# Hybrid decoder block on one core: the gates' first columns and dt from the plain transposed x, 1/rms on their products

## The chip, the cores and the metric

The kernel runs on one core of one Trainium2 chip. The metric is device time in microseconds (us) of one execution; less is better. Five engines work beside each other, each on its own queue in order: TensorE (PE, matmuls), VectorE (DVE), ScalarE (ACT), GpSimd (POOL) and SyncE (SP, which here only issues DMAs). They meet through semaphores. TensorE's clock has two levels, 1.2 and 2.4 GHz; the profile gives the granted level as a share of the higher one.

## What is computed

The reference is one decoder layer for a sequence of 256 tokens with 1024 channels. Cut to what matters here:

```python
hn = rmsnorm(x, norm1_w)                 # x * rsqrt(mean(x^2) + eps) * norm1_w
proj = hn @ w_in                         # z, x/B/C, dt, q, k, v, gates
z, xbc_raw, dt_raw, q, k, v, g_raw = jnp.split(proj, IN_OFFSETS, axis=-1)
dt = softplus(dt_raw + dt_bias)          # per token and head (32 heads)
gates = jax.nn.sigmoid(g_raw + b_gate)   # 2 x 1024 columns
merged = g_ssd * (y_ssd @ w_ssd_proj) + g_att * (y_att @ w_att_proj)
```

`y_ssd` comes from a chunked state-space scan that needs `dt`, `y_att` from causal attention over the 256 tokens. Then follow an output projection, a convolutional feed-forward layer and a last normalisation. Since 1/rms is one factor per token, `rmsnorm(x, w) @ W` is the same as `(x * w) @ W` with each token's row of the product multiplied by 1/rms.

## The kernel before

All matmuls over weights are done in three parts to keep float32's precision: a weight tile is split into `hi` (ScalarE, line 93, a rounded copy) and `lo` (VectorE, line 94, the rest), an activation likewise into a pair, and PE adds hi·hi, hi·lo and lo·hi. The weights arrive as units of 1 MB (128 partitions, 8 slices of 256 columns) in an order fixed by the list `seq`; `load_to` issues the transfers on SP into three `raw` buffers, `next_unit` hands out unit i, requests unit i+2 and splits unit i+1. A unit of 256 output columns is 48 matmuls of 128x256 (`mm_unit`, lines 148 to 150). The gates are made in blocks of 512 columns from two units each: 48 matmuls of 128x512 with the tokens as rows (`mm_tok`, lines 165 to 167), cut in four quarters of 12 by `u_gate`, a generator that is stepped with `next(gate)`.

The start (lines 225 to 260): x comes in token layout in three transfers, ScalarE squares and sums it (line 244), VectorE makes 1/rms by Newton steps (`rms_rstd`, lines 180 to 191), puts it on the diagonal of a matrix `dg` (line 249), and PE transposes and scales x in one by 16 float32 matmuls with `dg` (line 254). The norm weight is put on by `scaled_pairs` (lines 218 and 220), and eight pairs `hn` come out. Before x is there PE runs 14 matmuls on ones (line 71).

The order of PE's work is the program's order. For the first group g = 0 it is: `u_bc(0)` (B and C columns, then convolution and SiLU), `dt_mm` (32 columns of dt, line 460), `u_x(0)`, `dt_chain` (softplus on VectorE, lines 474 to 495), `u_qk(0)`, `u_z(0)`, `dt_sums` (cumulative sums, line 499), the first quarter of the gates, `dt_turn` (line 507; the sums go out to DRAM and come back spread over all partitions as `acsB`), `s_cb(0)` (lines 345 to 359: the decay matrix `mx`), the other quarters of the gates with `s_xt(0)` between, and then group 1: `u_bc(1)`, `s_y(0)` (line 381, the first product with `mx`), `u_x(1)` and so on. ScalarE's, VectorE's and GpSimd's orders are set by a planner at compile time from priorities in program order and its own costs. GpSimd does next to nothing: some memsets, and two products at the end (line 727).

Of the kernel before, what the change touches and what calls it, by code (L numbers as in the profile page):

```python
# [8 lines left out]
F32 = mybir.dt.float32  # L9
# [3 lines left out]
ALU = mybir.AluOpType  # L13
PSUM = bass.MemoryType.PSUM
DRAM = bass.MemoryType.DRAM
PE_ONLY = {mybir.EngineType.PE}

# [18 lines left out]
WARM = 14  # L36


def block_kernel(tc, xtok_d, par_d, nf_d, con_d, rope_d, wdt_d, win_d, wgate_d, bg_d, watt_d, wssd_d, wout_d, wup_d, wdn_d, out_d):
# [3 lines left out]
    with st:  # L43
# [12 lines left out]
        wdt = const.tile([P, KD, NH], F32, name="wdt")  # L56
        con3 = con[:, 0 : 7 * P].rearrange("p (a b) -> p a b", b=P)
# [15 lines left out]
        def col(c):  # L73
            return par[:, c : c + 1]
# [10 lines left out]

        def split_unit(raw, nk=KD):

            halves = []
            for k0 in range(0, nk, 4):
                n = min(4, nk - k0)  # L90
                hi = wpool.tile([P, 4, 256], F32R, tag="hi", bufs=4, name="hi")
                lo = wpool.tile([P, 4, 256], F32R, tag="lo", bufs=4, name="lo")
                nc.scalar.activation(hi[:, :n], raw[:, k0 : k0 + n], AF.Copy)  # L93
                nc.vector.tensor_tensor(lo[:, :n], raw[:, k0 : k0 + n], hi[:, :n].bitcast(F32), op=ALU.subtract)  # L94
                halves.append((hi, lo, n))
            return halves
# [72 lines left out]
        def mm_tile():  # L169
            return ps_mm.tile([P, 2, T], F32, tag="mm", bufs=3, name="mm")  # L170
# [59 lines left out]
        XCUT = ((0, 0, D), (1, 0, D // 2), (1, D // 2, D))  # L230
        for c, a, b in XCUT:
            nc.sync.dma_start(xtok[:, c, a:b], xtok_d[:, c, a:b])
        nc.sync.dma_start(con[:, 0:P], con_d[:, 0:P])
        nc.sync.dma_start(par, par_d)
        load_to(1)
        nc.sync.dma_start(con[:, P:], con_d[:, P:])
        nc.sync.dma_start(wdt, wdt_d)
        nc.sync.dma_start(rope, rope_d)
        ssum = work.tile([P, 3], F32, name="ssum")
        rstd1 = work.tile([P, 2], F32, name="rstd1")  # L240
        with tc.high_priority():
            junk = inp.tile([P, D], F32, name="junk")
            for i, (c, a, b) in enumerate(XCUT):
                nc.scalar.activation(junk[:, a:b], xtok[:, c, a:b], AF.Square, accum_out=ssum[:, i : i + 1])
            rms_rstd(rstd1[:, 0:1], ssum[:, 0:1], 1.0 / D)
            rms_rstd(rstd1[:, 1:2], ssum[:, 1:2], 1.0 / D, more=ssum[:, 2:3])
            dg = inp.tile([P, 2, P], F32, name="dg")
            for c in range(2):
                nc.vector.tensor_scalar(dg[:, c], ident, rstd1[:, c : c + 1], None, op0=ALU.mult)
            xps = [ps_mm.tile([P, 2, T], F32, tag="mm", bufs=3, name="xps") for _ in range(2)]  # L250
            xps += [ps_s.tile([P, 2, T], F32, tag="at", bufs=2, name="xps") for _ in range(2)]
            for c in range(2):
                for k in range(KD):
                    nc.tensor.matmul(xps[k // 2][:, k % 2, c * P : c * P + P], xtok[:, c, k * P : k * P + P], dg[:, c],
                                     start=True, stop=True)
            hn = []
            for i in range(4):
                hn += scaled_pairs("hn", [xps[i][:, m] for m in range(2)], [col(C_N1 + 2 * i + m) for m in range(2)])
# [196 lines left out]
        def dt_mm():  # L455
            with tc.manual_schedule(engines=PE_ONLY):
                for k in range(KD):
                    for i in range(2):
                        j = NH * (k % 2 * 2 + i)
                        nc.tensor.matmul(ps_dt[j : j + NH, 0, :], wdt[:, k], hn[k][:, i, :].bitcast(F32),  # L460
                                         start=(k < 2), stop=(k >= KD - 2))
# [10 lines left out]
        def dt_chain():  # L472
# [3 lines left out]
            for c in range(2):  # L476
                nc.tensor.matmul(ps[:, 0, c * NH : c * NH + NH], dtp[:, c * P : c * P + P], sel, start=True, stop=True)
            nc.vector.tensor_tensor(r3(0), ps[:, 0, 0 : 2 * NH].rearrange("p (c h) -> p c h", c=2),
                                    b3(par[:, C_DTB : C_DTB + NH]), op=ALU.add)
# [45 lines left out]
        gates = const.tile([P, 2, 2 * D], F32, name="gates")  # L525

        def u_gate(j):

            cols = slice(512 * j, 512 * j + 512)
            ps = [mm_tile(), mm_tile()]  # L530
            for k0 in (0, 4):
                hv = next_unit()
                mm_tok(ps, hv[:1], hn, k0, KD)
                yield
                mm_tok(ps, hv[1:], hn, k0 + 2, KD)
                if not k0:
                    yield
            for c in range(2):
                gt = gates[:, c, cols]
                nc.vector.tensor_tensor(gt, flat(ps[c]), gt, op=ALU.add)  # L540
                nc.scalar.activation(gt, gt, AF.Tanh, scale=0.5)
            yield

        for g in range(NG):
            if g:
                u_bc(g)
                s_y(g - 1)
                u_x(g)
                a_s(g - 1)
            u_qk(g)  # L550
            if g == 0:
                for c in range(2):
                    tc.keep_in_program_order(nc.scalar.dma_start(gates[:, c], bg_d.partition_broadcast(P)))
                u_z(g)
                dt_sums()
                gate = u_gate(0)
                next(gate)
                dt_turn()
                load_acs(0)
                s_cb(g)  # L560
                next(gate)
                s_xt(g)
                next(gate)
                next(gate)
            elif g % 2:
                s_cb(g)
                s_st(g - 1)
                u_v(g)
                a_t(g - 1)
                u_z(g)  # L570
                s_xt(g)
                a_o(g - 1)
                s_pb(g - 1)
            else:
                s_cb(g)
                s_st(g - 1)
                u_z(g)
                a_t(g - 1)
                s_xt(g)
                gate = u_gate(g // 2)  # L580
# [246 lines left out]
```

## Time and profile before

| | us |
|---|---|
| median of 3 runs | 615.52 |
| lowest and highest run | 615.33, 616.99 |
| the profiled execution | 617.0 |
| its span, first to last instruction | 615.2 |
| PE busy in it | 595.5 |
| VectorE busy | 464.0 |
| ScalarE busy | 358.5 |
| GpSimd busy | 4.1 |

The profiled execution is as long as the highest of the three runs. 1.8 us of it lie outside its span. Matmuls are pipelined and their ends are modelled in the profile, so the pace of PE is better read from the distance of the starts than from the durations.

### The profile page before, as it was taken

How to read it: one execution, taken by the hardware profiler on the slowest of the kernel's cores; microseconds unless marked ns; L12 is line 12 of the kernel's file. 1: busy time of each engine (PE TensorE's matmuls, PEld its weight loads, DVE VectorE, ACT ScalarE, POOL GpSimd, SP SyncE). 2: the span in 40 equal slices, each digit the busy share in tenths (PEclk: the TensorE clock that was granted, in tenths of full speed). 3: DMA queues.
4: the chain of work that ended last, by engine and by line, in shares of the span. 5: the costliest groups of instructions: out<-in, count | busy, mean ns of one | idle time of the engine just before them, and what ended most of it. 6: DMA issues, size and time to landing. Idle time of an engine off the chain costs nothing.

```text
span 615.2 us, 10606 instructions
## 1 busy us (share of the span) xinstructions
PE 595.5 (97%) x4194; PEld 545.0 (89%) x4194; DVE 464.0 (75%) x896; ACT 358.5 (58%) x648; POOL 4.1 (1%) x8
## 2 busy tenths in 40 slices
PE   8998999999999999999999999998999999999994
PEld 7897899989999899988988788788999999998883
DVE  4876898968979698896986546667888888884633
ACT  5645967649586595855846333455555555553431
POOL 0000000000000000000000000000000000000100
PEclk8999999999999999999999999999999999999998
DMA  8667364464544555345363765544455455455611
GB/s 331 218 232 271 120 211 171 150 222 138 192 142 165 205 169 177 138 151 202 136 208 94 279 196 174 185 161 152 164 206 172 171 206 174 172 205 162 214 35 69
DMA packets 17746, 109.78 MB, mean 178 GB/s; under 512 B 2176, under 2 KB 2592, under 8 KB 5664
## 3 DMA queue, kind: packets, MB, share of 16 engines
q1 hardware_dynamic: 15120, 100.15, 46.8%
q10 hardware_dynamic: 2576, 8.95, 4.2%
q8 instruction: 33, 0.54, 0.3%
q14 instruction: 17, 0.14, 0.1%
HBM read 107.49 MB, written 1.08 MB: 176 GB/s over the span
## 4 chain that ended last, share of the span: by engine, by line
PE 93%; DVE 3%; ACT 2%; DMA 1%; issue 1%; DVEq 0%; ACTq 0%
PE mm L148 17%; PE mm L149 16%; PE mm L150 16%; PE mm L167 10%; PE mm L165 10%; PE mm L166 10%; PE py L381 2%; PE mm L327 1%; PE mm L329 1%; PE mm L328 1%; PE s_ps L410 1%; DVE lo L94 1%; PE po L447 1%; PE pt_ps L433 1%; PE pb L210 1%
## 5 line engine op out<-in xcount | busy, mean ns | idle before, releaser
L93 ACT ACTIVATE hi<-raw 128x1024 fp32r<-128x1024 f32 x186 | 195.9, 1060 | 184.1 <-PE mm L167 83.8
L94 DVE TENSOR_TENSOR lo<-raw,hi 128x1024 fp32r<-128x1024 f32 x186 | 226.6, 1226 | 90.8 <-ACT hi L93 90.6
L148 PE MATMUL mm<-hn,hi 128*128 128x256 f32 x512 | 147.3, 288 | 0.0
L149 PE MATMUL mm<-hn,hi 128*128 128x256 f32 x512 | 145.0, 283 | 0.4 <-DVE hn L220 0.4
L150 PE MATMUL mm<-hn,lo 128*128 128x256 f32 x512 | 144.8, 283 | 0.0
L148 PEld LDWEIGHTS mm<-hn,hi 128*128 128x128 f32 x512 | 98.0, 191 | 4.1 <-issue 3.6
L149 PE MATMUL mm<-xw,hi 128*128 128x256 f32 x352 | 99.7, 283 | 1.0 <-DVE xw L220 1.0
L148 PE MATMUL mm<-xw,hi 128*128 128x256 f32 x352 | 99.8, 283 | 0.6 <-ACT xw L218 0.6
L150 PE MATMUL mm<-xw,lo 128*128 128x256 f32 x352 | 99.6, 283 | 0.0
L149 PEld LDWEIGHTS mm<-hn,hi 128*128 128x128 f32 x512 | 98.1, 192 | 0.9 <-DVE hn L220 0.8
L150 PEld LDWEIGHTS mm<-hn,lo 128*128 128x128 f32 x512 | 98.1, 192 | 0.0
L149 PEld LDWEIGHTS mm<-xw,hi 128*128 128x128 f32 x352 | 67.6, 192 | 1.2 <-DVE xw L220 1.2
L148 PEld LDWEIGHTS mm<-xw,hi 128*128 128x128 f32 x352 | 67.6, 192 | 0.8 <-ACT xw L218 0.8
L150 PEld LDWEIGHTS mm<-xw,lo 128*128 128x128 f32 x352 | 67.6, 192 | 0.0
L272 DVE SCALAR_TENSOR_TENSOR cacc<-mm,par,cacc 128x255 f32<-128x255 f32 (+2 forms) x96 | 44.2, 475 | 3.0 <-ACT cacc L268 2.9
L165 PE MATMUL mm<-hi,act 128*128 128x512 f32 x88 | 34.2, 389 | 0.0
L166 PE MATMUL mm<-lo,act 128*128 128x512 f32 x88 | 34.2, 389 | 0.0
L167 PE MATMUL mm<-hi,act 128*128 128x512 f32 x88 | 34.2, 389 | 0.0
L166 PE MATMUL mm<-lo,hn 128*128 128x512 f32 x64 | 25.0, 391 | 1.7 <-DVE lo L94 1.7
L165 PE MATMUL mm<-hi,hn 128*128 128x512 f32 x64 | 25.8, 404 | 0.0
L165 PE MATMUL mm<-hi,yn 128*128 128x512 f32 x64 | 25.3, 396 | 0.0
L167 PE MATMUL mm<-hi,hn 128*128 128x512 f32 x64 | 25.1, 392 | 0.0
(170 smaller groups left out, 939.6 us busy)
## 6 DMA issues: line engine op xcount, KB each, us to landing
raw<-in_win_dram SPq DMA_DIRECT2D x35, 1024.0 KB
raw<-in_wup_dram SPq DMA_DIRECT2D x22, 1024.0 KB
raw<-in_wdn_dram SPq DMA_DIRECT2D x10, 1024.0 KB
raw<-in_wgate_dram SPq DMA_DIRECT2D x8, 1024.0 KB
raw<-in_wssd_dram SPq DMA_DIRECT2D x8, 1024.0 KB
acsB<-acsT_d ACTq DMA_DIRECT2D x8, 512.0 KB
raw<-in_watt_dram SPq DMA_DIRECT2D x4, 1024.0 KB
raw<-in_wout_dram SPq DMA_DIRECT2D x4, 1024.0 KB
```

The lines of the kernel that those rows point to most:

```text
L93: nc.scalar.activation(hi[:, :n], raw[:, k0 : k0 + n], AF.Copy)
L94: nc.vector.tensor_tensor(lo[:, :n], raw[:, k0 : k0 + n], hi[:, :n].bitcast(F32), op=ALU.subtract)
L148: nc.tensor.matmul(ps[m], wh, xh, start=a, stop=False)
L149: nc.tensor.matmul(ps[m], wh, xl, start=False, stop=False)
L150: nc.tensor.matmul(ps[m], wl, xh, start=False, stop=z)
L165: nc.tensor.matmul(o, xh, wh, start=(k0 + k == 0), stop=False)
L166: nc.tensor.matmul(o, xh, wl, start=False, stop=False)
L167: nc.tensor.matmul(o, xl, wh, start=False, stop=(k0 + k == nk - 1))
L210: nc.tensor.matmul(pb[:, 0, c * P : c * P + P], y[:, c : c + 1].to_broadcast([P, P]), ident, start=True, stop=True)
L272: nc.vector.scalar_tensor_tensor(acc[:, s:], src[:, m, : T - s], w(m, 3 - s), acc[:, s:], op0=ALU.mult, op1=ALU.add)
L327: nc.tensor.matmul(ps[:, c, :], xh, hi[:, kk], start=(k == 0 and c == 0), stop=False)
L381: nc.tensor.matmul(o, xt[:, c, r, :], rhs, start=(c == 0), stop=(c == 1))
```

## The change

PE's first work is now the first gate block, and the normalised x is made later. In detail:

- Transfers: the identity and the norm weight go out first, on ScalarE's queue. On SP come the first half of x's columns, the first gate unit in three parts, the second half of x, the second gate unit in two parts, then `wdt`, the other parameters, the other constants and `rope`. The two gate units stand at the front of `seq`.
- x is transposed plainly (`x_turn`), split with the norm weight alone on it (`x_split`, pairs `xr`), and ScalarE, VectorE and PE follow a written order there (`IN_ORDER`), in which the splits of x and of the gate units alternate (`w_split`), and the squares (`x_square`) and `rms_rstd` come late.
- The four quarters of gate block 0 and `dt_mm` use `xr`. 1/rms is put on by one operand of the VectorE instruction that adds the bias, for the gates and for dt (there two instructions instead of one).
- GpSimd adds hi and lo of `xr` back to full values (`norm1_full`, 8 additions of 128x256), and when 1/rms is there and PE has spread it over the partitions (`rms_bcast`), multiplies them by it (8 products of 128x256); `split_pair` then makes the pairs `hn` (`norm1`).
- The order of group 0 is gates, `dt_mm`, `dt_chain`, `u_bc(0)`, `dt_sums`, `u_x(0)`, `dt_turn`, `u_qk(0)`, `s_cb(0)`, `u_z(0)`, `s_xt(0)`. The gates' bias is loaded for 512 columns first and for the others later. The matmuls on ones go from 14 to 10.

```diff
-WARM = 14
+WARM = 10
...
+        for d, h in ((con[:, 0:P], con_d[:, 0:P]), (par[:, 0:C_NW], par_d[:, 0:C_NW])):
+            nc.scalar.dma_start(d, h)
...
+        nc.sync.dma_start(xhalf(xtok, 0), xhalf(xtok_d, 0))
+        for k0, k1 in ((0, 2), (2, 4), (4, 8)):
+            nc.sync.dma_start(raw0[:, k0:k1], seq[0][0][:, k0:k1])
+        nc.sync.dma_start(xhalf(xtok, 1), xhalf(xtok_d, 1))
+        for k in (0, 4):
+            nc.sync.dma_start(raw1[:, k : k + 4], seq[1][0][:, k : k + 4])
...
+        def x_split():
+            k = len(xr)
+            xr.extend(scaled_pairs("xr", [xps[k // 2][:, k % 2]], [col(C_N1 + k)]))
...
+        def w_split(u, k0, step):
+            hi, lo = split_tiles()
+            for k in range(0, 4, step):
+                x_split()
+                split_part(raws[u][:, k0 + k : k0 + k + step], hi[:, k : k + step], lo[:, k : k + step])
+            units[u].append((hi, lo, 4))
+
+        def norm1_full():
+            for k in range(KD):
+                nc.gpsimd.tensor_tensor(full[:, k], xr[k][:, 0, :].bitcast(F32),
+                                        xr[k][:, 1, :].bitcast(F32), op=ALU.add)
+
+        def norm1():
+            nc.scalar.activation(rb1, rms_bcast(rstd1), AF.Copy)
+            for k in range(KD):
+                nc.gpsimd.tensor_tensor(full[:, k], full[:, k], rb1, op=ALU.mult)
+                hn.append(new_pair("hn"))
+                split_pair(hn[k], full[:, k])
...
+                    nc.vector.scalar_tensor_tensor(gt, flat(ps[c]), rstd[:, c : c + 1], gt, op0=ALU.mult, op1=ALU.add)
...
         st.enter_context(tc.manual_schedule(engines=PE_ONLY))
-        u_bc(0)
+        gate = u_gate(0, xr, rstd1)
+        with tc.manual_schedule(engines=IN_ORDER):
+            x_turn(0)
+            units.extend(([], []))
+            w_split(0, 0, 2)
+            next(gate)
+            w_split(0, 4, 2)
+            x_turn(1)
+            next(gate)
+            x_square(0)
+            w_split(1, 0, 4)
+            x_split()
+            x_square(1)
+            w_split(1, 4, 4)
+            x_split()
+            rms_rstd(rstd1, ssum[:, 0], 1.0 / D, more=ssum[:, 1])
+        load_bias(0, 512)
+        norm1_full()
         dt_mm()
-        u_x(0)
+        next(gate)
         dt_chain()
+        norm1()
+        next(gate)
...
+            else:
+                u_bc(0)
+                dt_sums()
+                u_x(0)
+                dt_turn()
+                load_acs(0)
             u_qk(g)
             if g == 0:
+                load_bias(512, 2 * D)
+                s_cb(g)
                 u_z(g)
-                dt_sums()
-                gate = u_gate(0)
-                next(gate)
-                dt_turn()
-                load_acs(0)
-                s_cb(g)
-                next(gate)
                 s_xt(g)
-                next(gate)
-                next(gate)
```

## Rows read from the trace of the kernel before

**Rows 1.** The page's first part: busy time of each engine, its share of the span and its instructions.
```profile
PE 595.5 (97%) x4194; PEld 545.0 (89%) x4194; DVE 464.0 (75%) x896; ACT 358.5 (58%) x648; POOL 4.1 (1%) x8
```

**Rows 2.** Busy time by stretches of the first 70 us. Columns: the stretch and its length; busy us and instructions of PE, PEld, DVE, ACT, POOL; the granted clock of TensorE; the mean busy share of the DMA engines; GB/s.
```profile
0.00:5.00 5.00, 3.95 (x18) 3.95 (x19) 0.17 (x1) 1.49 (x2) 0.20 (x4) 1.00 0.58 168
5.00:10.00 5.00, 3.01 (x20) 2.82 (x19) 3.42 (x25) 3.66 (x8) 0.00 (x0) 0.86 1.03 395
8.60:12.00 3.40, 3.40 (x17) 3.40 (x17) 2.43 (x9) 0.84 (x1) 0.00 (x0) 0.50 1.06 420
10.00:15.00 5.00, 5.00 (x35) 4.82 (x35) 2.67 (x5) 2.44 (x6) 0.00 (x0) 0.80 1.04 428
15.00:20.00 5.00, 4.61 (x39) 4.41 (x38) 5.00 (x9) 3.42 (x7) 0.00 (x0) 1.00 0.75 272
20.00:25.00 5.00, 5.00 (x59) 3.94 (x58) 3.59 (x7) 3.60 (x6) 0.00 (x0) 1.00 0.65 210
25.00:30.00 5.00, 5.00 (x44) 5.00 (x43) 3.92 (x7) 2.82 (x5) 0.99 (x2) 1.00 0.62 203
30.00:40.00 10.00, 10.00 (x86) 10.00 (x84) 9.63 (x28) 4.24 (x9) 0.00 (x0) 1.00 0.41 125
40.00:50.00 10.00, 8.32 (x44) 6.73 (x43) 5.19 (x9) 4.87 (x6) 0.00 (x0) 1.00 0.78 311
50.00:60.00 10.00, 10.00 (x66) 9.08 (x65) 6.46 (x7) 5.92 (x15) 0.00 (x0) 1.00 0.85 280
60.00:70.00 10.00, 8.34 (x74) 7.54 (x72) 7.68 (x14) 8.55 (x17) 0.00 (x0) 1.00 0.35 143
```

**Rows 3.** The timeline of PE from the start to the first dt product. Columns: start us, us, engine, line, operation, tiles, shapes, count, and the idle time ahead of it.
```profile
1.05 5.35 PE L71 MATMUL warm<-ones 128*128 128x128 f32 x28 [1.05 <-DVE ones L64]
...
8.39 5.47 PE L254 MATMUL xps<-dg,xtok 128*128 128x128 f32 x32 [1.99 <-DVE dg L249]
...
13.62 0.36 PE L148 MATMUL mm<-hn,hi 128*128 128x256 f32 x1
...
20.43 1.93 PE L460 MATMUL ps_dt<-hn,wdt 128*32 128x256 f32 x32
```

**Rows 4.** The timeline of PE from `dt_turn` to the first product with `mx`; columns as in Rows 3.
```profile
43.41 0.38 PE L507 MATMUL ps_t<-con,acs 128*32 128x128 f32 x2
...
44.20 0.48 PE L165 MATMUL mm<-hi,hn 128*128 128x512 f32 x1
...
46.80 0.40 PE L167 MATMUL mm<-hi,hn 128*128 128x512 f32 x1
47.04 0.60 PE L366 MATMUL pxt<-con,xs 128*128 128x128 f32 x4
...
49.55 0.50 PE L166 MATMUL mm<-lo,hn 128*128 128x512 f32 x1 [1.68 <-DVE lo L94]
...
54.94 0.28 PE L148 MATMUL mm<-hn,hi 128*128 128x256 f32 x1
...
60.57 0.28 PE L150 MATMUL mm<-hn,lo 128*128 128x256 f32 x1
62.51 1.52 PE L381 MATMUL py<-mx,xt 128*64 128x256 f32 x16 [1.66 <-DVE mx L359]
```

**Rows 5.** The timeline of ACT and then of DVE in the first 20 us: what x and the first weights ended, and the six later instructions of `scaled_pairs` on either engine; columns as in Rows 3.
```profile
5.09 1.06 ACT L244 ACTIVATE junk<-xtok 128x1024 f32<-128x1024 f32 x1 [2.86 <-DMA xtok<-in_xtok_dram]
...
8.38 1.06 ACT L93 ACTIVATE hi<-raw 128x1024 fp32r<-128x1024 f32 x1 [0.66 <-DMA raw<-in_win_dram]
...
14.23 2.29 ACT L218 ACTIVATE hn<-xps,par 128x256 fp32r<-128x256 f32 x6
...
15.52 2.44 DVE L220 SCALAR_TENSOR_TENSOR hn<-xps,par,hn 128x256 fp32r<-128x256 f32 x6
```

**Rows 6.** The timeline of DVE with the first and the last link of the chain that makes 1/rms of the first 128 tokens (nine instructions start from 6.27 up to the last link); then groups of instructions by line and shape, the first three in the first 80 us, the last over the whole span, with count, busy us and mean ns.
```profile
6.27 0.15 DVE L180 TENSOR_SCALAR rv<-ssum 128x1 f32<-128x1 f32 x1 [5.28 <-ACT junk L244]
...
8.06 0.28 DVE L249 TENSOR_SCALAR dg<-con,rstd 128x128 f32<-128x128 f32 x1
...
L540 DVE TENSOR_TENSOR gates<-mm,gates 128x512 f32<-128x512 f32 x2 | 1.4, 688 | 1.6 <-PE mm L167 1.6
...
L489 DVE SCALAR_TENSOR_TENSOR dtw<-dtw 128x64 f32<-128x64 f32 x6 | 1.3, 221 | 0.1
...
L244 ACT ACTIVATE junk<-xtok 128x512 f32<-128x512 f32 x2 | 1.2, 620 | 0.0
...
L174 DVE TENSOR_TENSOR act<-fth,act 128x256 fp32r<-128x256 f32 x22 | 9.2, 418 | 0.0
```

**Rows 7.** The timeline of DVE near the end of the span, where GpSimd works too: two splits of the same shape; then GpSimd's two products there, with the shortest, mean of the two and longest duration in ns and their starts.
```profile
577.66 1.23 DVE L94 TENSOR_TENSOR lo<-raw,hi 128x1024 fp32r<-128x1024 f32 x1 [0.30 <-ACT hi L93]
...
580.43 1.95 DVE L94 TENSOR_TENSOR lo<-raw,hi 128x1024 fp32r<-128x1024 f32 x1 [1.39 <-ACT hi L93]
...
L727 POOL TENSOR_TENSOR x<-x,nfb x2: 1288/1478/1669, 578.4 to 580.0; 128x512 f32<-128x512 f32 x2
```

**Rows 8.** The timeline of DVE: the first and the last instruction of `dt_chain`'s work on dt, and the product that completes `mx` of group 0.
```profile
28.72 0.23 DVE L478 TENSOR_TENSOR dtw<-ps_dt,par 128x64 f32<-128x64 f32 x1 [0.66 <-PE ps_dt L477]
...
39.75 0.23 DVE L495 TENSOR_TENSOR dtw<-dt,nega 128x64 f32<-128x64 f32 x1
...
60.70 1.76 DVE L359 TENSOR_TENSOR mx<-mx,cb 128x1536 f32<-128x1536 f32 x1 [2.68 <-ACT mx L357]
```

More of the change, by code (lines that the diff above doesn't have):

```diff
@@ L16 @@
 PE_ONLY = {mybir.EngineType.PE}
+IN_ORDER = {mybir.EngineType.PE, mybir.EngineType.Activation, mybir.EngineType.DVE}
 P = 128
@@ new lines, in block_kernel, with load_bias @@
+        gates = const.tile([P, 2, 2 * D], F32, name="gates")
+        def load_bias(a, b):
+            tc.keep_in_program_order(
+                nc.scalar.dma_start(gates[:, :, a:b], bg_d[None, a:b].partition_broadcast(P).to_broadcast([P, 2, b - a])))
+        xr, hn = [], []
+        xps = [ps_s.tile([P, 2, T], F32, tag="at", bufs=2, name="xps") for _ in range(2)]
+        xps += [ps_mm.tile([P, 2, T], F32, tag="mm", bufs=3, name="xps"),
+                ps_s.tile([P, 2, T], F32, tag="acc", bufs=1, name="xps")]
@@ new lines, in block_kernel, with x_turn @@
+        ssum = work.tile([P, 2, 2], F32, name="ssum")
+        rstd1 = work.tile([P, 2], F32, name="rstd1")
+        junk = inp.tile([P, 512], F32, name="junk")
+        rb1 = inp.tile([P, T], F32, name="rb1")
+        full = inp.tile([P, KD, T], F32, name="full")
+        def x_turn(i):
+            for k in range(4 * i, 4 * i + 4):
+                for c in range(2):
+                    nc.tensor.transpose(xps[k // 2][:, k % 2, c * P : c * P + P], xtok[:, c, k * P : k * P + P], ident)
+        def x_split():
+            k = len(xr)
+            xr.extend(scaled_pairs("xr", [xps[k // 2][:, k % 2]], [col(C_N1 + k)]))
@@ L477, in dt_chain @@
                 nc.tensor.matmul(ps[:, 0, c * NH : c * NH + NH], dtp[:, c * P : c * P + P], sel, start=True, stop=True)
-            nc.vector.tensor_tensor(r3(0), ps[:, 0, 0 : 2 * NH].rearrange("p (c h) -> p c h", c=2),
-                                    b3(par[:, C_DTB : C_DTB + NH]), op=ALU.add)
+            for c in range(2):
+                nc.vector.scalar_tensor_tensor(r3(0)[:, c], ps[:, 0, c * NH : c * NH + NH], rstd1[:, c : c + 1],
+                                               par[:, C_DTB : C_DTB + NH], op0=ALU.mult, op1=ALU.add)
             nc.scalar.activation(dtw[:, 1], dtw[:, 0], AF.Abs)
@@ L509, in dt_turn, with u_gate @@
             nc.scalar.dma_start(acsT_d, acsT)
-        st.enter_context(tc.manual_schedule(engines=PE_ONLY))
-        u_bc(0)
+        def u_gate(j, act, rstd=None):
+            cols = slice(512 * j, 512 * j + 512)
+            ps = [mm_tile(), mm_tile()]
+            for k0 in (0, 4):
+                hv = next_unit()
+                mm_tok(ps, hv[:1], act, k0, KD)
+                yield
+                mm_tok(ps, hv[1:], act, k0 + 2, KD)
+                if not k0:
+                    yield
+            for c in range(2):
+                gt = gates[:, c, cols]
+                if rstd is None:
+                    nc.vector.tensor_tensor(gt, flat(ps[c]), gt, op=ALU.add)
+                else:
+                    nc.vector.scalar_tensor_tensor(gt, flat(ps[c]), rstd[:, c : c + 1], gt, op0=ALU.mult, op1=ALU.add)
+                nc.scalar.activation(gt, gt, AF.Tanh, scale=0.5)
+            yield
+        st.enter_context(tc.manual_schedule(engines=PE_ONLY))
+        gate = u_gate(0, xr, rstd1)
[16 more added lines that the diff above has]
+        norm1_full()
         dt_mm()
-        u_x(0)
+        next(gate)
         dt_chain()
+        norm1()
+        next(gate)
         st_in.close()
@@ L523, in block_kernel @@
             swaps.append(s)
[L525 to L542, printed above, removed]
         for g in range(NG):
@@ L579, in block_kernel @@
                 s_xt(g)
-                gate = u_gate(g // 2)
+                gate = u_gate(g // 2, hn)
                 next(gate)
```

62 lines of the change are left out of this document (26 added, 36 removed).

## The prediction

> **What bounds the kernel now.** I read the page's first part, then busy time by stretches, then PE's timeline up to the point where old and new order meet again, then the other engines there. PE is busy 97% of the span [rows 1], so a change pays only where PE waits or has no work yet. The stretches [rows 2] show where: the first 15 us, 40 to 50 (8.32 of 10 us busy) and 60 to 70 (8.34). PE's first useful matmul starts at 13.62; before it lie the matmuls on ones and the 16 of `dg`, which begin only when 1/rms is there [rows 3]. The two later gaps are 1.68 us for a `lo` and 1.66 us for `mx` [rows 4]. VectorE is the engine to watch: it is full in 15 to 20 and 30 to 40 (9.63 of 10), with 40.1 us busy in the first 60 [rows 2].
>
> As a mark I take the first matmul of `s_y(0)`, at 62.51 before [rows 4]. Up to it both kernels do the same matmuls on weights, only in another order; behind it the program is the same. What the mark gains is what the kernel gains, unless a backlog of VectorE is left behind it.
>
> **Part by part: the start.** The first SP transfer is again 512 KB; before, its data was used at 5.09 [rows 5]. Beside it now go 76 KB on ScalarE's queue, at 168 GB/s [rows 2] 0.45 us; between nothing and that, I take x at 5.4, and 5.9 for the first instruction of ScalarE. Four matmuls on ones fewer cost nothing: ten end near 1.05 + 10/14 of 5.35 = 4.9 [rows 3], before x is there. If PE's clock falls, it costs what rows show: in 8.60 to 12.00 it was granted at 0.50 (1.2 GHz), after PE had been idle for 1.99 us [rows 2, 3]. New idle time lies before `dt_mm`, so up to 1.7 us of such a loss stays in the range.
>
> ScalarE then sets the pace: 8 splits of x at 2.29/6 = 0.38 [rows 5], four parts of the first unit and four squares at 0.62 [rows 6], two of 1.06 [rows 5]: 3.0 + 2.5 + 2.5 + 2.1 = 10.1 us, so to 16.0. The transfers keep up: 3.2 MB must be there for the last of these weights; 0.84 MB move in the first 5 us, 1.98 in the next, then 428 GB/s [rows 2], which gives 10.9 and with 0.8 us of landing 11.7, while ScalarE wants them near 15. The next unit stands behind the constants (5.1 MB, so near 16.2) and is wanted no earlier. VectorE follows ScalarE by a `lo` of 1.23 [rows 7] and a 0.41 [rows 5], 17.2 with the handovers; GpSimd's additions beside it may hold it up, I put 0.4: 17.6. Then `rms_rstd` has 13 instructions at 0.20 (nine in 8.06 - 6.27 = 1.79 [rows 6]): 1/rms at 20.2, against 8.06 for the first tokens before [rows 6]. That is the price of the change: 1/rms and `hn` come later.
>
> PE meanwhile does half of the gates and most of `dt_mm`, waits for the last pair, and goes on at 17.6: a gate quarter 12 x 0.236 = 2.8 (11 steps in 46.80 - 44.20 [rows 4]), dt and the spreading of 1/rms, new, 0.9: 21.3. ScalarE's copy ends at 21.9, and the last quarter runs to 24.1 under the first products. GpSimd's product of 128x512 took 1.29 us at best [rows 7], so half as many columns 0.64 and eight 5.2. `u_bc(0)` uses 0.72 us of PE per slice (6 x 0.12, 47 steps in 60.57 - 54.94 [rows 4]), so GpSimd alone keeps up. For PE alone `u_x(0)` could start at 24.1 + 5.8 + 0.5 = 30.4.
>
> **VectorE is later than that.** From 20.2 it has, before PE can start `u_x(0)`: the `lo` of the unit for `u_bc(0)`, 2.4; 18 instructions of `dt_chain` at 0.22 [rows 6], 4.0 (`dt_sums` stands in PE's queue ahead of `u_x(0)`, so all of PE waits for it); 8 new `lo` of `hn` at 0.42 [rows 6], 3.4; two gate sums, 1.4 [rows 6]; half of the next unit's `lo`, 1.2. That is 12.4: to 32.6.
>
> Beside that GpSimd reads and writes SBUF, which before it did only at the end. There a split that ran beside its product took 1.95 instead of 1.23, and the product that began inside the other split took 1.67 instead of 1.29 [rows 7]. So the two engines hold each other up. For the eight products the bounds are 0 (they fall beside instructions that don't mind) and all 5.2; I take the row's share, 0.72 of 1.29, so 0.56 x 5.2 = 2.9. `u_x(0)` then starts at 35.5. The Trainium skill goes further (SBUF — State Buffer, "Who interferes with whom"): a VectorE instruction with two inputs in SBUF and a GpSimd one that reads SBUF exclude each other for the whole instruction. The rows agree in kind, since either side lost time; by the rule alone the sum would be that of the second rival.
>
> From there to the mark PE has four units (`u_x`, `u_qk`, `u_z`, `u_bc(1)`), 192 x 0.12 = 23.0, and small matmuls, 44.20 - 43.41 and about half of the 0.60 of `s_xt`, whose modelled end lies under what follows, 1.1 [rows 4]: 24.1. Mark at 59.6, so 2.9 us gained. Is `mx` ready by then? `dt_turn` comes 17 us ahead of the mark against 19.1 (62.51 - 43.41) before, in which ScalarE and VectorE were held up by other work; a way by DRAM, 5 us of ScalarE and the 1.76 of VectorE [rows 8] fit. VectorE's total to the mark was 40.1 + 1.8 = 41.9 [rows 2, 8]; the new pairs and the smaller pieces make it some 44.5, which leaves 15 us idle: enough, if the order is good.
>
> The median is 615.52 and the profiled run 617.0. The sum is a difference inside the profiled run; on it 614.1 would follow. I put it on the median: 615.52 - 2.9 = 612.6.
>
> **The rivals.**
> First, GpSimd is well covered and VectorE's order good: `u_x(0)` starts between 30.4 and 32.6, the mark lies at 54.5 to 56.7, the time at 607.5 to 609.7. For it: VectorE's instructions on PSUM and the tiny ones lie among the others. Against: VectorE has no slack there.
> Second, the engines shut each other out fully: 32.6 + 5.2 = 37.8, mark at 61.9, gain 0.6, time 614.9. For it speak both pairs of [rows 7]; against it, that products while `hn` is awaited cost VectorE nothing. It is the rule of the page named above, and its time comes out of these rows.
> Third, the other side: `dt_chain` strewn between other work, as before, where from first to last instruction it took 39.98 - 28.72 = 11.3 us [rows 8] for 4.0 of work. From 21 that is 32.3; with all of GpSimd's 5.2 37.5, and the next unit's whole `lo` behind it, 2.4: 39.9, mark at 64.0, 1.5 us slower: 617.0. It decides once `u_x(0)` starts after 62.51 - 24.1 = 38.4. Against it: before, convolutions lay in between, which now come after.
> That the change doesn't do what it says has one form: VectorE's or ScalarE's queue holds an instruction that waits for the late parameters before the first splits. It would add to the third.
>
> **How the numbers follow.** Forecast 0.46, its own range 610.5 to 613.6; first rival 0.20, second 0.22, third 0.12. A measurement here tells some 0.3% (1.85 us) from no change. Faster, under 613.7: 0.46 + 0.20 = 0.66. Same: the second, 0.22. Slower: the third, where it goes past 617.4 with the clock's loss, and its like: 0.12. The range leaves out the best half of the first rival and the worst of the third: 608.3 to 616.9.
>
> **What would show it.** Right: PE's first matmul with weights near 7, a pause before the last products of `dt_mm`, 1/rms near 20, `u_x(0)` at 34 to 37 behind VectorE, `lo` instructions and GpSimd's products longer than alone, the mark near 59.6. Wrong: `u_x(0)` right behind `u_bc(0)` (first rival), after 38.4 (third), or a mark that comes early with new gaps behind it, which would mean that the backlog was only passed on.

## The result, and the profile after

| | before | after |
|---|---|---|
| median | 615.52 us (615.33 to 617.01, 5 runs) | 622.70 us (621.72 to 624.08, 5 runs) |
| profiled execution, its span | 617.0, 615.2 | 624.08, 622.0 |
| first matmul of `s_y(0)` (the mark) | 62.51 | 66.86 |

After is 1.0108 times before, 95% interval 1.0091 to 1.0124: slower by 1.1%, where 612.6 was forecast and 616.9 was the upper end of the range. TensorE's wait ahead of the marked matmul, 1.66 us in [rows 4], is gone, and the matmul still comes 4.35 us later. Each ratio is against runs of before taken beside it; these lie in two groups, near 615.4 and near 617.0 us, in changing shares (their median was 616.79 beside the first four experiments).

The first part of after's page:
```profile
PE 597.9 (96%) x4174; PEld 545.3 (88%) x4174; DVE 468.4 (75%) x899; ACT 362.2 (58%) x661; POOL 17.3 (3%) x24
```
PE is busy for 2.4 us more [rows 1], in a span that is 6.8 longer, so most of the loss is waiting, and the rest slower matmuls. Busy time by stretches of after, columns as in [rows 2]:
```profile
30.00:40.00 10.00, 4.43 (x32) 4.16 (x31) 9.98 (x28) 6.57 (x10) 0.99 (x2) 0.92 0.31 106
38.50:45.30 6.80, 6.41 (x30) 6.44 (x31) 3.63 (x10) 1.10 (x3) 0.00 (x0) 0.50 0.52 195
427.60:431.00 3.40, 3.40 (x18) 3.40 (x18) 1.58 (x8) 0.00 (x0) 0.00 (x0) 0.50 0.33 135
```
Against [rows 2] one stretch stands out: from 30 to 40 PE is busy 4.43 of 10 us (10.00 before), and VectorE 9.98. Right behind it lies a stretch in which TensorE's clock was granted at 0.50, its level of 1.2 GHz (called half clock from here on). Another lies near 428, in the feed-forward part.

PE's timeline says what it waited for; columns as in [rows 3]:
```profile
6.62 0.49 PE L177 MATMUL mm<-hi,xr 128*128 128x512 f32 x1 [0.65 <-ACT hi L93]
...
18.49 0.62 PE L508 MATMUL ps_dt<-xr,wdt 128*32 128x256 f32 x2 [1.13 <-DVE xr L232]
...
25.55 0.28 PE L160 MATMUL mm<-hn,hi 128*128 128x256 f32 x1
...
29.45 0.39 PE L161 MATMUL mm<-hn,hi 128*128 128x256 f32 x1 [1.40 <-DVE hn L186]
...
38.89 0.66 PE L548 MATMUL ps_a<-dtw,con 128*128 128x64 f32 x2 [5.57 <-DVE dtw L544]
...
39.74 0.56 PE L160 MATMUL mm<-hn,hi 128*128 128x256 f32 x1
40.52 0.41 PE L160 MATMUL mm<-hn,hi 128*128 128x256 f32 x1
```
The front is much as forecast: first product with weights at 6.62, a pause of 1.13 us before dt's last pair. Then the longest wait of the kernel: PE stands 5.57 us before `dt_sums` (L548), because the last instruction (link) of `dt_chain` (L544) ends only at 38.75. `u_x(0)` starts at 39.74, past the 38.4 that the prediction named as the deciding point, and its first matmuls run at half the clock: 0.41 us each where the profile shows 0.28 at 25.55.

Why the chain ends so late is seen on VectorE, in its timeline:
```profile
21.07 0.16 DVE L203 SCALAR_TENSOR_TENSOR rstd<-ra,rstd 128x2 f32<-128x2 f32 x1
21.15 2.36 DVE L94 TENSOR_TENSOR lo<-raw,hi 128x1024 fp32r<-128x1024 f32 x2
23.43 0.40 DVE L527 SCALAR_TENSOR_TENSOR dtw<-ps_dt,rstd,par 128x32 f32<-128x32 f32 x2
24.75 0.50 DVE L186 TENSOR_TENSOR hn<-full,hn 128x256 fp32r<-128x256 f32 x1 [0.92 <-ACT hn L185]
...
28.23 0.19 DVE L531 TENSOR_SCALAR dtw<-dtw 128x64 f32<-128x64 f32 x1 [1.22 <-ACT dtw L530]
28.34 0.72 DVE L540 TENSOR_SCALAR dtw<-dtw 128x64 f32<-128x64 f32 x1
28.98 0.41 DVE L186 TENSOR_TENSOR hn<-full,hn 128x256 fp32r<-128x256 f32 x1
...
33.15 0.21 DVE L538 SCALAR_TENSOR_TENSOR dtw<-dtw 128x64 f32<-128x64 f32 x1
33.29 1.21 DVE L94 TENSOR_TENSOR lo<-raw,hi 128x1024 fp32r<-128x1024 f32 x1
34.42 0.21 DVE L538 SCALAR_TENSOR_TENSOR dtw<-dtw 128x64 f32<-128x64 f32 x1
34.56 1.21 DVE L94 TENSOR_TENSOR lo<-raw,hi 128x1024 fp32r<-128x1024 f32 x1
35.69 0.21 DVE L538 SCALAR_TENSOR_TENSOR dtw<-dtw 128x64 f32<-128x64 f32 x1
35.83 1.21 DVE L94 TENSOR_TENSOR lo<-raw,hi 128x1024 fp32r<-128x1024 f32 x1
36.96 0.21 DVE L538 SCALAR_TENSOR_TENSOR dtw<-dtw 128x64 f32<-128x64 f32 x1
37.10 0.47 DVE L320 SCALAR_TENSOR_TENSOR cacc<-mm,par,cacc 128x255 f32<-128x255 f32 x1
...
38.54 0.21 DVE L544 TENSOR_TENSOR dtw<-dt,nega 128x64 f32<-128x64 f32 x1
```
Work of some 4 us takes from 23.43 to 38.75, 15.3 us, in two parts. Up to 28.23 the chain waits for its two links on ScalarE (L529 and L530), and ScalarE's timeline shows these behind the `hi` parts of `hn`, which wait for GpSimd's products one by one:
```profile
26.76 0.42 ACT L185 ACTIVATE hn<-full 128x256 fp32r<-128x256 f32 x1 [0.47 <-POOL full L303]
27.08 0.24 ACT L529 ACTIVATE dtw<-dtw 128x64 f32<-128x64 f32 x1
...
27.95 0.24 ACT L530 ACTIVATE dtw<-dtw 128x64 f32<-128x64 f32 x1
```
VectorE is idle for 2.5 us in this part, in four waits for ScalarE. From 28.34 on it is never idle, but the planner has put one other instruction between nearly every two links: pairs of `hn`, gate sums, three splits (`lo`) of 1.21 each and pieces of convolutions of 0.47. The pairs of `hn` are wanted by PE before `dt_sums`; what comes from 31.70 on, the gate sums and all behind them, is not.

### The profile page after: what moved, and what is told of

It reads as the page before. It is cut to its first block, busy times and chain, and to the rows that moved or that the text cites. A ratio compares the mean times of both kernels' runs of the same rounds, so it can differ in the third digit from the quotient of the medians.

```text
span 622.0 us, 10596 instructions
## 1 busy us (share of the span) xinstructions
PE 597.9 (96%) x4174; PEld 545.3 (88%) x4174; DVE 468.4 (75%) x899; ACT 362.2 (58%) x661; POOL 17.3 (3%) x24
## 4 chain that ended last, share of the span: by engine, by line
PE 86%; DVE 4%; ACT 2%; issue 1%; DMA 1%; ACTq 1%; POOL 0%; DVEq 0%
PE mm L160 16%; PE mm L161 15%; PE mm L162 15%; PE mm L177 10%; PE mm L179 10%; PE mm L178 10%; PE py L429 2%; DVE lo L94 1%; PE mm L376 1%; PE mm L375 1%; PE mm L377 1%; PE s_ps L458 1%; PE po L495 1%; PE pt_ps L481 1%; DMA acsB<-acsT_d 1%
## 5 line engine op out<-in xcount | busy, mean ns | idle before, releaser
L94 DVE TENSOR_TENSOR lo<-raw,hi 128x1024 fp32r<-128x1024 f32 (+1 forms) x188 | 228.4, 1221 | 99.9 <-ACT hi L93 99.8
L93 ACT ACTIVATE hi<-raw 128x1024 fp32r<-128x1024 f32 (+1 forms) x188 | 196.1, 1050 | 183.4 <-PE mm L161 81.3
L160 PEld LDWEIGHTS mm<-hn,hi 128*128 128x128 f32 x512 | 99.3, 194 | 3.7 <-issue 3.4
L161 PEld LDWEIGHTS mm<-hn,hi 128*128 128x128 f32 x512 | 99.4, 194 | 1.9 <-DVE hn L186 1.6
L161 PEld LDWEIGHTS mm<-xw,hi 128*128 128x128 f32 x352 | 68.3, 194 | 1.2 <-DVE xw L232 1.2
L160 PEld LDWEIGHTS mm<-xw,hi 128*128 128x128 f32 x352 | 68.3, 194 | 0.8 <-ACT xw L230 0.8
L177 PE MATMUL mm<-hi,yn 128*128 128x512 f32 x64 | 25.3, 396 | 0.0
L178 PE MATMUL mm<-lo,yn 128*128 128x512 f32 x64 | 24.9, 390 | 0.0
L179 PE MATMUL mm<-hi,yn 128*128 128x512 f32 x64 | 24.9, 390 | 0.0
L402 ACT ACTIVATE mx<-acsB,acs 128x128 f32<-128x128 f32 x64 | 22.1, 392 | 4.4 <-DMA swap<-qkraw 3.4
```

Source lines behind the costliest of these rows:

```text
L93: nc.scalar.activation(hi, raw, AF.Copy)
L94: nc.vector.tensor_tensor(lo, raw, hi.bitcast(F32), op=ALU.subtract)
L160: nc.tensor.matmul(ps[m], wh, xh, start=a, stop=False)
L161: nc.tensor.matmul(ps[m], wh, xl, start=False, stop=False)
L177: nc.tensor.matmul(o, xh, wh, start=(k0 + k == 0), stop=False)
L178: nc.tensor.matmul(o, xh, wl, start=False, stop=False)
```

## Experiments

The theory at the start: PE's wait for the strewn chain, and the half clock that follows, are the whole loss, 7.2 us. The rival: the loss is another's (the additions' hold-up of VectorE, or a lateness of `mx` that the wait only covers). Each expectation says what its two sides are. The edits are shown condensed.

**The sums behind `u_x(0)`.** So `dt_sums` no longer stands ahead of a unit that doesn't need it.
```
             u_bc(0)
-            dt_sums()
             u_x(0)
+            dt_sums()
-            dt_turn(); load_acs(0)      # were ahead of u_qk(0)
             u_qk(0)
+            dt_turn(); load_acs(0)
```


> The changed kernel with dt_sums behind u_x(0) and dt_turn with load_acs behind u_qk(0) in PE's order; same work. Theory A (the loss is PE's 5.57 us wait for dt_chain's end ahead of dt_sums, and the half clock that follows it, some 3 us): u_x(0) starts at 33.5 to 35 at full clock, the first s_y(0) near 59 to 60 instead of 66.9, time 613 to 615.5. Rival B (VectorE has more work than time, so the wait only moves to another place ahead of s_y(0)): s_y(0) after 64, time 620 to 623.

Measured: 620.88 us (1.0069, 1.0049 to 1.0090). `u_x(0)` starts at 33.46, `dt_sums` is at 40.45 without a wait, and PE is through with everything ahead of the mark at 59.6. There it stands 3.39 us for `mx` and goes on at 63.00, at half clock from 62.93 to 66.35. The front is the theory's, the time the rival's: with the first wait gone, a second one shows. ScalarE's timeline says why `mx` is late:
```profile
47.51 1.22 ACTq L357 DMA_DIRECT2D swap<-qkraw  x1
48.76 0.64 ACTq L358 DMA_DIRECT2D swap<-qkraw  x1
...
50.80 0.45 ACTq L558 DMA_DIRECT2D acsT_d<-acsT  x1
...
52.40 0.35 ACTq L347 DMA_DIRECT2D acsB<-acsT_d  x1
...
56.59 0.69 ACT L402 ACTIVATE mx<-acsB,acs 128x128 f32<-128x128 f32 x2 [3.29 <-DMA acsB<-acsT_d]
```
The sums go out to DRAM behind the issue of q and k's swaps (four, 3.1 us of ScalarE's queue), and `mx` waits for their return.

**The chain first.** `dt_chain()` put under the planner's high priority.

> The changed kernel with dt_chain at high priority, PE's order untouched. The planner still puts one other VectorE instruction between two links of the chain, but three weight splits fewer stand ahead of its end. Theory A: dt_sums 1.5 to 4 us earlier than 38.9, time 618 to 621. Rival B (VectorE's total counts, not its order): within 1 us of 622.7.

620.87 us (1.0076, 1.0056 to 1.0097), within the theory's range. ScalarE's links come sooner, so that VectorE goes on with the chain at 24.93 instead of 28.23, 3.3 us earlier. Of this some 2 us go again, since two links and two pairs of `hn` now run beside GpSimd's products:
```profile
26.89 0.75 DVE L534 TENSOR_TENSOR dtw<-dtw 128x64 f32<-128x64 f32 x1
27.57 0.97 DVE L186 TENSOR_TENSOR hn<-full,hn 128x256 fp32r<-128x256 f32 x1
```
In after such links took 0.21, and the pairs 0.41 to 0.68. The other instructions still stand between the links. So the wait falls only from 5.57 to 3.74 and `dt_sums` comes at 37.63, 1.3 earlier. Half clock lasts 3.4 us instead of 6.8, the mark is at 64.37.

**The clock kept.** Ahead of `dt_sums`, 24 matmuls of the ones into a tile that nothing reads, so that PE isn't idle in its wait.

> The changed kernel with 24 more matmuls of 128x128 on ones between u_bc(0) and dt_sums, where PE waits anyway; they add no wait if they end by 38.9. If the half clock behind the wait costs on its own: the granted clock stays 1.00 from 38 to 46, dt_sums starts at 38.9 as before, s_y(0) near 64 and the time near 619.5. If the clock is no cost of its own (u_x(0) would wait for VectorE anyway): within 1 us of 622.7.

619.89 us (1.0059, 1.0041 to 1.0077), as expected. `dt_sums` is at 38.93, as in after, the mark at 64.32. The stretch that after ran at half clock:
```profile
38.50:45.30 6.80, 6.60 (x56) 6.43 (x55) 5.00 (x11) 1.90 (x4) 0.00 (x0) 1.00 0.64 242
```
With nothing changed but the clock, the mark comes 2.5 us earlier, although PE now waits 0.40 for `mx` there: so much the half clock costs. The median falls by 2.8; the half clock near 428, which after's profile has, isn't in this one either.

**No additions.** GpSimd's additions left out (its products take one half of x; the output lacks the other).

> The changed kernel without GpSimd's 8 additions: hn is made from the high part of x alone, so the output is only near the reference. VectorE's splits in the first 18 us were held up by some 1.8 us beside them. Theory A: 1/rms and all behind it 1.5 to 2 us earlier, the wait for dt_chain stays near 5.5 us, time 620 to 621.5. Rival C (GpSimd's hold-up of VectorE is the main cause): the wait shrinks below 3 us, time under 618.

622.44 us (1.0100, 1.0085 to 1.0116), outside both sides' ranges. VectorE's splits are back at 1.23 and 1/rms comes at 20.4, 0.8 us earlier, but the chain ends at 38.9: VectorE waits 1.42 us instead of 0.92 for ScalarE's part of the first `hn`, and a later pair takes 0.99 instead of 0.41 beside GpSimd's products. PE waits 2.00 us for that pair, and this profile has a stretch at half clock in `u_bc(0)` that after's hasn't:
```profile
31.20:34.60 3.40, 3.40 (x19) 3.40 (x18) 3.40 (x10) 2.67 (x4) 0.98 (x2) 0.50 0.01 2
```
So the wait ahead of `dt_sums`, at 39.03, is shorter (4.06) only because PE comes to it later; the mark is at 67.32. The additions' hold-up of VectorE is real and not the cause. The products stayed in, so this run says nothing against theirs.

**The turn inside `u_qk(0)`.** As with the sums late, but the transposes of the sums and the load of `acsB` stand between the halves of `u_qk(0)`, so that they leave ScalarE's queue ahead of the swaps. With it, the same under high priority for the chain, and one with both steps right behind `u_x(0)`.
```
-            mm_unit(ps, hv, hn)
+            mm_unit(ps, hv[:1], hn, last=False)
+            if g == 0:
+                dt_turn(); load_acs(0)
+            mm_unit(ps, hv[1:], hn, first=False, k0=4)
```


> As e1_sums_late (dt_sums behind u_x(0)), with dt_turn and load_acs between the two halves of u_qk(0), so that the sums' way over DRAM stands ahead of the q/k row swaps on ScalarE's queue. Theory A2 (three waits in a row: dt_chain, then the way of the sums to mx over ScalarE's queue; each hides the next): PE reaches s_y(0) near 60 as in e1, mx is there by 58, no wait at s_y(0), no half clock, time 612.5 to 614.5, faster than before. Rival B (ScalarE or VectorE has no room, mx comes near 62.5 whatever the order): s_y(0) waits 2 us or more, time 617 or above.

> e6 with dt_chain at high priority as in e2. Theory A2: dt_chain no longer ends late for dt_sums at 40, so the priority is worth nothing more, and u_bc(0) loses what VectorE's links take from hn: within 1 us of e6. If VectorE's order ahead of 34 matters in itself: 1 us or more to either side of e6.

> dt_sums and dt_turn both right behind u_x(0): PE waits there for VectorE's copy of the sums, 0.9 to 1.8 us. Theory A2: that wait is all that is lost against e6; s_y(0) near 61 to 61.5 with no wait, time 613.5 to 616. Rival B: s_y(0) after 62.5, time 617 or above.

With the turn inside `u_qk(0)` alone the time is 616.21 us (1.0008, 0.9992 to 1.0025): the whole loss is gone, but nothing is gained. PE is ready at 59.07 and waits 2.20, as the rival has it, though the time is under the rival's; ScalarE's part of `mx` ends at 57.46, but VectorE has the swap ahead of `mx`'s product in its queue:
```profile
58.12 0.69 DVE L367 TENSOR_TENSOR swap<-swap,rope 128x512 f32<-128x512 f32 x1 [4.08 <-DMA swap<-qkraw]
58.85 0.69 DVE L368 TENSOR_TENSOR qk<-qk,swap 128x512 f32<-128x512 f32 x1
59.46 1.75 DVE L411 TENSOR_TENSOR mx<-mx,cb 128x1536 f32<-128x1536 f32 x1
```
That is a third wait. With the priority as well it is 616.49 (1.0014), the same. With both steps right behind `u_x(0)` it is 622.40 (1.0105), which neither theory nor rival had so high: ScalarE waits 2.44 for `acsB`, then issues the swaps, and so is late with the next unit's weights, for which PE stands 2.80 and then runs at half clock from 60.5 to 67.3. Where the turn stands is worth 6 us, by what it lets ScalarE's queue do first.

**The third wait.** From the turn inside `u_qk(0)`: (1) `mx`'s product ahead of the swap on VectorE; (2) the second load of the bias behind the second load of `acsB`, instead of ahead of `mx`, and with it, which its expectation doesn't name, the swap's two VectorE instructions behind `s_cb(0)` in program order, so later in the planner's priorities; (3) as (2), and the swaps of group 0 issued from GpSimd's queue.

> The kernel with the turn of the sums between the halves of u_qk(0), and one thing more: VectorE does mx's product of group 0 ahead of the swap's two instructions in its queue, instead of behind them. Theory A (the last of three waits is VectorE's queue, which stands 4.08 us for the swap's DMA although mx of ScalarE is done at 57.46): the product runs from about 57.5 to 59.2, the first s_y(0) matmul is at 59.3 instead of 61.27, PE waits about 0.2 us there instead of 2.20, and the time is 616.2 - 2.0 = 614.2 us (613.5 to 615.0), under the 615.5 of the kernel before. Rival B (what is won at the mark is given back later, by the next wait or by the clock): s_y(0) at 59.3 all the same, but the last s_y and the time do not move with it, 616.0 to 616.8 us.

> The kernel with the turn of the sums between the halves of u_qk(0), VectorE's order as it was there, and only the second load of the gates' bias (1536 columns, 1.09 us of issue on ScalarE's queue at 51.76) moved from ahead of mx to behind the second load of acsB. Theory A (the bias's packets share the queue with the swaps and hold their landing up, 58.1 for an issue that ends at 51.7): the swaps land 3 us earlier or more, VectorE is ready when ScalarE's mx ends at about 57.4, s_y(0) at 59.3 and the time 614.2 us (613.5 to 615.0). Rival B (the swaps and acsB land late because of the weight stream or because of their own way, not because of the bias): landing at 57.5 to 58.5 as before, s_y(0) at 61 and the time 616.2 us (615.5 to 616.8).

> As the run with the bias later, and also the four swap DMAs of group 0 are issued from GpSimd's queue instead of ScalarE's, so that ScalarE issues nothing but acsT and acsB between u_x(0) and mx. Theory A (each of the waits ahead of mx is a queue's): mx starts when acsB lands and the swaps land by about 54, so that s_y(0) waits for nothing but its own inputs: 59.1 to 59.4, time 613.9 us (613.0 to 614.8). Rival B (acsB and the swaps are late by their own way through memory): ScalarE still idle some 4 us for acsB, s_y(0) 60.5 or later, time 615.5 us or more.

(1) did to the mark what was expected, and not to the time. PE's timeline:
```profile
59.47 1.52 PE L443 MATMUL py<-mx,xt 128*64 128x256 f32 x16 [0.30 <-DVE mx L419]
...
62.41 0.39 PE L163 MATMUL mm<-hn,lo 128*128 128x256 f32 x1 [0.98 <-DVE lo L95]
```
The mark is 1.80 us earlier than in the run before it, but a split that now stands behind the product costs PE 0.98 in the next unit, and from the second `s_y` on only 0.37 is left (96.17 against 96.54). The time is 617.61 (1.0033, 1.0020 to 1.0046). (2) left the swaps' landing where it was (58.0; rival B). But the splits behind `mx`'s product moved back in VectorE's order (from 61.73 to 64.23), and PE waited 2.49 for `mx` and 2.10 for a split, with half clock from 62.5 to 69.3: 620.32 (1.0075, 1.0049 to 1.0101). Which of its two edits moved them, the run can't say. (3) has the swaps landed at 56.75 and the mark at 59.89 with 0.56 of wait, nearer to its theory's 59.4 than to the rival's 60.5, but 616.54 us (1.0004, 0.9992 to 1.0015), the rival's; its profiled execution, 615.54, shows no half clock between the front and the last 10 us. Its other runs reach from 613.97 to 617.18.

**What scatters the runs.** The remaining spread was as large as the gain looked for. Several profiles show a half-clock stretch of 3.4 us near 421 (after: near 428), right behind two short waits for `xw`, the activations of the feed-forward part; others show none. So the edits made so far were put together (the sums late, the turn inside `u_qk(0)`, the swaps from GpSimd, the bias later, the product first), and matmuls of the ones laid into those two waits; beside it, before with the same matmuls alone.
```
                 transposed(1)
+                for _ in range(24):
+                    nc.tensor.matmul(busy[:, 0, 0:P], ones, ones, start=True, stop=True)
                 mm_unit(ps, hv[1:], xw2, first=False, k0=4)
```


> The changed kernel with the edits of the runs before put together: the sums behind u_x(0), their turn between the halves of u_qk(0), the swaps of group 0 issued by GpSimd, the second load of the bias behind the second acsB, mx's product ahead of the swap's turn on VectorE; and 24 matmuls of the ones (into a tile that nothing reads) behind the last transposes of x2, where TensorE waits 0.57 and 0.98 us for xw and where some profiles show half a clock for 3.4 us right after. Theory A (the change does bring the mark forward by about 3 us once the waits behind it are gone, and what scatters the runs by 1.7 us is the clock after the waits for xw): first s_y(0) at 59.2 to 59.6, no half clock between there and the last stage in the profile, all runs in one group, time 613.5 to 614.6 us, under the 615.5 of before. Rival B (the scatter has another source, and the front's gain does not reach the end): the time 615.5 to 616.5 us, two groups of runs 1.6 us apart as in the runs before.

> The kernel before with the same 24 matmuls of the ones behind the last transposes of x2, and nothing else. It says what these do without the change. Theory A (the two groups of before's runs, 615.4 and 616.9, come from its front, where the profile of before shows half a clock from 8.6 to 12.0 us): no difference, 615.5 us, still two groups. Rival B (they come from the waits for xw at 421 us, as in the changed kernels): one group, 615.4 us. In both cases the run with all waits gone is to be measured against this one.

617.74 us (1.0029, 1.0019 to 1.0039) and 618.75 us (1.0048, 1.0033 to 1.0063): both slower, for the 24 were too many. From PE's timeline of before with them:
```profile
60.91 1.52 PE L381 MATMUL py<-mx,xt 128*64 128x256 f32 x16 [1.66 <-DVE mx L359]
...
418.49 5.52 PE L697 MATMUL busy<-ones 128*128 128x128 f32 x48
```
They ran as 48 instructions, 5.52 us where some 2 were free. But two things came out. Between the two the change is 1.0 us faster. And this profile of before has its mark at 60.91, not at 62.51: the stretch from 8.60 to 12.00, at half clock in [rows 2], ran at full clock in it:
```profile
8.60:12.00 3.40, 3.40 (x31) 3.40 (x32) 2.62 (x11) 1.94 (x4) 0.00 (x0) 1.00 1.04 412
```
So both were run once more with 6 of these matmuls, which fit.

> The run with all waits gone, with 6 instead of 24 extra matmuls of the ones: the 24 ran as 48 instructions in 5.52 us where the waits for xw left room for some 2, so that both kernels that had them paid about 3.2 us; 6 are 12 instructions of 0.115 us, 1.4 us, and fit. Theory A (the front of the change is worth the 1.45 us by which its first s_y(0) at 59.46 lies ahead of the 60.91 of the kernel before where that shows no half clock in its front, and nothing behind the mark takes it): one group of runs, 614.2 to 614.7 us, 0.8 to 1.3 us under the 615.45 of before. Rival B (the front's gain does not reach the end, and the 1.0 us between the two runs with 24 matmuls was the matmuls' own): 615.2 us or more.

> The kernel before with the same 6 matmuls at that place, as the control. Theory A (they fit into the waits; the two groups of before's runs come from its front): 615.3 to 615.6 us in most runs, some at 616.9. Rival B (they come from the waits for xw at 421 us): one group. In both cases the run with all waits gone is 0.8 to 1.3 us shorter by theory A.

The control is before itself: 615.51 us (1.0000, 0.9988 to 1.0011), still with two groups of runs (7 from 615.38 to 615.57, 5 from 617.02 to 617.09). The other is 614.69 us (614.04 to 615.17, 12 runs, one group), **0.9976 of before (0.9967 to 0.9985)**: the one version that beats both kernels, by a quarter of a per cent. The last units ahead of its mark, and the waits for `xw`, in PE's timeline:
```profile
59.79 1.52 PE L444 MATMUL py<-mx,xt 128*64 128x256 f32 x16
...
417.59 1.50 PE L777 MATMUL busy<-ones 128*128 128x128 f32 x12
419.69 0.39 PE L162 MATMUL mm<-xw,hi 128*128 128x256 f32 x1 [0.47 <-DVE xw L233]
```

## Why the prediction was wrong

**What held.** The start: weights from 6.62 ("near 7"), dt's pause, the last gate quarter's end at 25.5 (24.1), and most of ScalarE's pace. 1/rms came at 21.2, not 20.2, for two reasons. ScalarE was through with the start at 16.7, not 16.0, having waited 0.75 and 0.27 us for two parts of the gate weights: "the transfers keep up" didn't hold in the first 10 us.
```profile
7.83 0.64 ACT L93 ACTIVATE hi<-raw 128x512 fp32r<-128x512 f32 x1 [0.75 <-DMA raw<-in_wgate_dram]
```
And GpSimd's additions held VectorE up by more than the 0.4 put down. In VectorE's timeline and, for the addition, GpSimd's,
```profile
8.49 0.69 DVE L94 TENSOR_TENSOR lo<-raw,hi 128x512 fp32r<-128x512 f32 x1 [0.81 <-ACT hi L93]
...
9.76 1.20 DVE L94 TENSOR_TENSOR lo<-raw,hi 128x512 fp32r<-128x512 f32 x1 [0.17 <-ACT hi L93]
...
9.66 0.75 POOL L297 TENSOR_TENSOR full<-xr 128x256 f32<-128x256 f32 x1 [1.05 <-DVE xr L232]
```
The same split takes 1.20 beside an addition, and 0.69 otherwise (0.69 too in the run without additions); later ones 1.45 and 1.69 (1.23 in [rows 7]). With GpSimd's products, six pairs of `hn` take 0.41 to 0.50 and two 0.68, and one link 0.72. That is some 1.2 us more than alone, where the forecast had put down 2.9 and the second rival 5.2: neither price is in this trace. That the products' hold-up doesn't decide the time follows from these lengths; no run left the products out. The rule of the Trainium skill that the prediction weighed (SBUF — State Buffer, "Who interferes with whom": for a whole instruction, the one that came first shuts the other out) fits the 0.51 more on a split with two inputs in SBUF, which began 0.10 us after the addition.

**The step that failed** is "VectorE is later than that": its 12.4 us, with GpSimd's 2.9 15.3, from 1/rms to the start of `u_x(0)`. In the trace VectorE takes from 21.2 to 38.75, 17.5 us, and `dt_sums` itself, for which the sum had no term, holds PE until 39.74. So `u_x(0)` starts 4.2 us later than the forecast 35.5: 1.0 for the late 1/rms, 2.2 for VectorE, 1.0 for `dt_sums`. PE had been through with `u_bc(0)` at some 33.3. The list counted what PE needs, as if VectorE did that first and never waited; it set aside the order. What stands in the trace besides the listed work is 3 x 1.21 of splits instead of 1.2, three pieces of convolutions of 0.47, and 2.5 us of waits for ScalarE (0.92, 0.20, 0.20, 1.22), whose links of the chain and `hi` parts stand behind GpSimd's products.

That is the **third rival**, "`dt_chain` strewn between other work", with a chance of 0.12. It put `u_x(0)` at 39.9. That the trace shows 39.74 is luck in part: the rival added 11.3 us of chain and all 5.2 of GpSimd's, the trace has 15.3 of chain with 1.2 of hold-up in it. The reason given against it, that the convolutions now come after, was wrong twice. Three pieces of `u_bc(0)` lie inside the chain. And before, splits had lain in the chain too, three of them; VectorE's timeline of before has
```profile
34.48 1.22 DVE L94 TENSOR_TENSOR lo<-raw,hi 128x1024 fp32r<-128x1024 f32 x1
...
36.93 0.22 DVE L489 SCALAR_TENSOR_TENSOR dtw<-dtw 128x64 f32<-128x64 f32 x1
37.07 1.22 DVE L94 TENSOR_TENSOR lo<-raw,hi 128x1024 fp32r<-128x1024 f32 x1
```
[Rows 8] showed the same chain at 11.3 us for 4.0 of work, under an order made in the same way; this was evidence on the planner, and it should have carried more.

**The clock's term was too small.** The third rival's mark was 64.0, and the trace has 66.86. "Up to 1.7 us" came from a half-clock stretch of 3.4 us. After 5.57 us of idle it was 6.8 us long, and the run with the clock kept prices it at 2.5 at the mark. From `u_x(0)` to the mark PE took 27.1 us instead of 24.1.

**"Is `mx` ready by then?" was answered yes, and wrongly.** The prediction compared lengths (17 us against 19.1). It didn't walk along ScalarE's queue. With PE's first wait gone, PE was at the mark at 59.6 and stood 3.39 us for `mx`, which waits for the sums' way behind the swaps; with the sums ahead of the swaps it stood 2.20, for VectorE's queue. That 59.6 is the forecast to the tenth is luck: `u_x(0)` started at 33.46 instead of 35.5, and from there PE took 26.1 us instead of 24.1, 0.98 of them a wait for a split. Each of the three waits was hidden by the one before it.

**The reference was 1.6 us off.** The forecast subtracted a gain measured on the profiled 617.0 from the median of 615.52. Before's two groups of runs lie 1.6 us apart, and so do its two marks, 62.51 and 60.91: of the two versions of before with extra matmuls, the one profiled in its shorter group shows full clock in the front, the one profiled in its longer group half clock from 9.0 to 12.4. Most of before's runs are of the shorter group. So with a mark at 59.6 the change could bring only 60.91 - 59.6 = 1.3 us against the median, or, as the prediction also worked out, 614.1 "on the profiled run". With the waits ahead of the mark gone the mark was at 59.79, and the time 614.69.

Summed from the profiled 617.0 with its mark: +4.35 at the mark, of which 2.5 is the clock's (the run with the clock kept) and the rest comes from the late `dt_sums`; +0.8 until the second `s_y` (102.76 against 97.59, +5.17), which stays until 425.98 against 420.81; +1.6 behind that, with the half clock near 428, to the spans' difference of 6.8. Against a before at full clock in the front (60.91) the loss at the mark is 5.95.

**What stays open.** The order that put `mx`'s product first has a median 1.4 us above that of the run it was made from, though its mark and its second `s_y` are earlier; the two intervals overlap, so it may be scatter. Its runs lie 1.7 to 3.2 us above their spans, before's 1.7 to 1.9; what the device does there, the trace doesn't show. What made one group of the last version's 12 runs is not shown either: beside (3) it has the matmuls in the waits for `xw` and `mx`'s product ahead of the swap, and no run has the matmuls alone. Whether the planner can be brought to keep the chain together at 4 us was not tried beyond high priority.

## What to carry to other kernels

Where a planner or queue sets the order, a sum of durations up to a deadline is a lower bound: price a chain of small dependent instructions at one long neighbour for each link, as the trace already shows for the same chain, follow its links on every engine, and don't put its consumer ahead of an engine's independent work. When a wait is removed, follow the next input of the same matmul through every in-order queue (issuing of DMAs included) before its gain is booked. And subtract a gain from a median only if the profile that it is measured on belongs to that median's group of runs.

## What the runs showed of the hardware that was not expected

- After 5.57 us of idle, TensorE's clock was granted at 0.50 for 6.8 us (38.5 to 45.3 in after); after 3.74 us for 3.4 (the chain first); with matmuls of the ones in the same wait not at all. A wait of 2.00 us was followed by 3.4 us at 0.50 without the additions (31.2 to 34.6), one of 2.20 us ahead of the mark by none with the turn inside `u_qk(0)`. After the short waits for `xw` (0.57 and 0.98 us) the profiles of four versions show 3.4 us at 0.50, those of others none. In before the stretch in the front comes and goes from one execution to the next (inferred from the 1.6 us between its runs and between its marks).
- A small VectorE instruction can last as long as GpSimd's beside it: `rv` of 128x2 took 0.72 at 18.54 in after, with an addition of 0.74 from 18.51 (0.16 without the additions), and one on 128x64 took 0.72 at 28.34 beside the products (0.19 just before it).
- The DMAs ahead of `mx` are slow to land for their size: in the run with the turn inside `u_qk(0)` the four swaps, of 16 KB each, were issued by 51.7 and used at 58.12; `acsB` (four rows of sums, spread over 128 partitions, 512 KB) was issued at 46.40 and used at 52.90. With the bias's 1.5 MB issued behind both, neither of these times from issue to use changed by more than 0.2.
